# Wider moving operands for the attention values, shorter stationary operands in three HGRN levels

## The chip, the cores and the metric

The kernel runs on one core of a Trainium2 chip. The metric is the device time of one launch in microseconds; times are given as the median of several runs. The engines are named as in the profile: PE (TensorE matmuls), PEld (its weight loads), DVE (VectorE), ACT (ScalarE), POOL (GpSimd) and SP (SyncE, which issues the DMAs here).

## What is computed

The reference is one layer of a decoder trunk on 256 tokens and 1024 channels. A normed input is projected to 3072 columns, which feed three groups of token mixers: a gated linear recurrence (LRU, 256 channels), an HGRN2 group (4 heads of 64) and an attention group (8 heads of 64). The three results are concatenated, projected back, added to the input, and passed through a squared-ReLU MLP.

```python
h = rms_norm(x, norm_mix[l])
z = jnp.einsum('bsd,de->bse', h, w_in[l])
a_x, a_y, b_q, b_f, b_i, b_g, c_q, c_k, c_v = jnp.split(z, split_at, axis=-1)
ya = rglru_group(a_x, a_y, ...)
yb = hgrn2_group(b_q, b_f, b_i, b_g, lower_bounds[l], hg_norm_w[l])
yc = moba_group(c_q, c_k, c_v)
y = jnp.concatenate([rms_norm(ya, ...), yb, rms_norm(yc, ...)], axis=-1)
x = x + jnp.einsum('bse,ed->bsd', y, w_out[l])
h = rms_norm(x, norm_mlp[l])
u = jnp.square(jax.nn.relu(jnp.einsum('bsd,df->bsf', h, w_ff1[l])))
x = x + jnp.einsum('bsf,fd->bsd', u, w_ff2[l])
```

With 256 tokens the attention has a single key block, so it is causal softmax attention with a linear bias. `c_v`, the values, are the last 512 of the 3072 columns.

## The kernel before, in words

**Arithmetic.** Each large product is made of three fp32r matmuls (`mm3`, lines 299 to 303): high half by high half, high by low, low by high. Every weight chunk of 1 MB (128 partitions of 2048 numbers) is loaded by SP into one of three `raw` buffers and split in two halves by `split_w` (line 96, `S_` in the plan): a cast on ACT (line 71), then a subtraction on DVE (line 72). The split's second half also issues the load three chunks ahead.

**Order.** Everything before the MLP is written out by hand. `slots` (line 830) is a list of 84 pieces of matmul work: 48 quarters of the input projection (`in_quarter`, four for each of 12 chunks), 32 parts of the output projection (`wout_part`) and 4 first parts of the MLP. Ahead of a slot stand the steps that `plan` (line 835) gives for it. Each engine runs its own instructions strictly in the order in which slots and steps issue them; semaphores keep data in order across engines. PSUM is eight banks, handed out first freed, first used (`mis`, line 48; `free`, line 61).

**Values of the attention.** Chunks 10 and 11 of the input projection (slots 40 to 47) are the two halves of the value columns, 256 columns each with all eight contraction tiles. The tokens are stationary and the weights move (line 313): for a quarter, four contraction tiles by three matmuls of 256 moving columns. Each chunk takes one bank; `at_v` (line 624) brings it out on ACT with two activations of 256 columns, through `z_tok` (line 243).

**Attention.** For each head, `at_mm` makes scores, `at_max` (DVE) adds the bias and takes the maximum, `at_exp` (ACT, lines 652 and 653) exponentiates, `at_nrm` (DVE, lines 667 and 669) divides, `at_tr` (PE, line 658) transposes the probabilities, `at_pt` (ACT, line 662) brings them out, and `at_av` (PE, lines 673 to 682) multiplies a pair of heads by the values. Then come `at_sq`, `at_sum`, `at_ss`, `at_rms`, `at_bc`, `at_y` and `at_split` for the group's norm. Pairs 0 and 1 of `at_av` stand ahead of slot 46, ahead of the transpose of head 7; pairs 2 and 3 stand ahead of slot 50. `at_ss` stands ahead of slot 53 and `at_bc`, which needs its result by way of DVE and POOL, ahead of slot 56.

**HGRN levels.** `hg_mm(L)` (lines 390 to 405) makes the attention of a block of tokens on the block before it, for L = 1, 2, ..., 64. It has eight products of 64 stationary rows by 128 stationary columns (keys) by 64 moving columns (queries), in f32; the trace shows each as two matmuls, so 16 a level. The two head halves use partitions 0 to 63 and 64 to 127. `hg_pred` reads the result; for L of 16 and more it reads rows `2*L*n` to `2*L*n + L`, so never the last L.

Of the kernel before, what the change touches and what calls it, by code (L numbers as in the profile page):

```python
# [11 lines left out]
AF = mybir.ActivationFunctionType  # L12
# [3 lines left out]
P = 128  # L16
S = 256
D = 1024
KT = D // P
# [13 lines left out]
def trunk_kernel(ctx: ExitStack, tc, x, x_t, w_in, w_out, w_ff1, w_ff2, small, hg_norm, norm_final, out):  # L33
    nc = tc.nc
    V, A, G, T = nc.vector, nc.scalar, nc.gpsimd, nc.tensor
# [12 lines left out]
    def mis(name):  # L48
        b = idle.pop(0)
        held[name] = (b,)  # L50
        return banks[:, b, :]

    def mis2(name):
        age = {b: n for n, b in enumerate(idle)}
        b = min((b for b in (0, 2, 4, 6) if b in age and b + 1 in age), key=lambda b: max(age[b], age[b + 1]))
        idle.remove(b)
        idle.remove(b + 1)
        held[name] = (b, b + 1)
        return banks[:, b:b + 2, :]

    def free(name):
        idle.extend(held.pop(name))

    def wt(name, shape, tag=None, bufs=None, dt=F32):
        return work.tile(shape, dt, name=name, tag=tag or name, bufs=bufs)
# [11 lines left out]
    NI = len(in_order)  # L77
# [9 lines left out]
    raw, hi_w, lo_w = {}, {}, {}  # L87
# [68 lines left out]
    hTh, hTl = hT[:, :, 0, :], hT[:, :, 1, :]  # L156
# [30 lines left out]
    for L in LEVELS:  # L187
        n = 64 // L
        m = const.tile([P, n, L], F32, name=f"lmask{L}")
# [24 lines left out]
    rx = wt("rx", [P, 2])  # L214
# [28 lines left out]
    def z_tok(i, dst, func=AF.Copy):  # L243
        for t in range(2):
            A.activation(dst[:, t, :], z[i][t], func, scale=rx[:, t:t + 1])
        free(f"z{i}")
# [52 lines left out]
    def mm3(o, l, r, first, last):  # L299
        (lh, ll), (rh, rl) = l, r  # L300
        T.matmul(o, lh, rh, start=first, stop=False)  # L301
        T.matmul(o, lh, rl, start=False, stop=False)  # L302
        T.matmul(o, ll, rh, start=False, stop=last)  # L303

    def in_mm(i, half, k):
        o = z[i][half]
        s_ = slice(half * 128, (half + 1) * 128)
        wh = hi_w[i].rearrange("p (k c) -> p k c", c=CW)[:, k, :]
        wl = lo_w[i].rearrange("p (k c) -> p k c", c=CW)[:, k, :]
        if in_order[i][1] == CH:  # L310
            mm3(o, (wh[:, s_], wl[:, s_]), (hTh[:, k, :], hTl[:, k, :]), k == 0, k == KT - 1)
        else:
            mm3(o, (hTh[:, k, s_], hTl[:, k, s_]), (wh, wl), k == 0, k == KT - 1)

    def in_quarter(i, q):
        if q == 0:
            if i < 2:
                z[i] = [mis(f"z{i}{b}")[:, 0:256] for b in range(2)]
            else:
                a = mis(f"z{i}")  # L320
                z[i] = [a[:, 0:256], a[:, 256:512], a]
        if i < 2:
            for k in (2 * q, 2 * q + 1):
                for half in range(2):
                    in_mm(i, half, k)
        else:
            for k in range(4 * (q % 2), 4 * (q % 2) + 4):
                in_mm(i, q // 2, k)
# [7 lines left out]
    kB = wt("kB", [P, 2, 256])  # L336
# [53 lines left out]
    def hg_mm(L):  # L390
        ps = ps_h[L] = mis2(f"lv{L}")
        halves = [slice(0, 64), slice(64, 128)]
        if L == 128:
            for hp in range(2):
                for par, r in enumerate(halves):
                    T.matmul(ps[:, par, hp * 128:(hp + 1) * 128], kB[r, hp, 0:128], qd[r, hp, 128:256],
                             start=True, stop=True)
            return
        for hp in range(2):
            for half in range(2):  # L400
                g = 2 * hp + half
                hs = slice(half * 128, (half + 1) * 128)
                for par, r in enumerate(halves):
                    rhs = qd[r, hp, hs].rearrange("p (n w) -> p n w", w=2 * L)[:, :, L:]
                    T.matmul(ps[:, par, g * 64:(g + 1) * 64], kB[r, hp, hs], rhs, start=True, stop=True)  # L405

    att_g = att_d.rearrange("p (g a) t -> p a g t", a=2)

# [205 lines left out]
    cv = wt("cv", [P, 2, 512])  # L614
# [6 lines left out]
    def at_k(g):  # L621
        zT(6 + 2 * g, ck[g])

    def at_v(g):
        z_tok(10 + g, cv[:, :, g * 256:(g + 1) * 256])

    def at_bias(h):
        sc_t[h] = wt("sc", [P, 384], tag="sc", bufs=3)
# [192 lines left out]
    def x1_ss():  # L821
        for t in range(2):
# [5 lines left out]
    nfb = wt("nfb", [P, D], tag="oc")  # L828
    S_ = split_w
    slots = [(in_quarter, i, 2 * h + q) for h in range(2) for i in range(2) for q in range(2)]  # L830
    slots += [(in_quarter, i, q) for i in range(2, NI) for q in range(4)]
    slots += [(wout_part, k, t, n) for k in range(4) for t, n in tn]
    slots += [(wout_part, k, t, n) for t, n in tn for k in range(4, 8)]
# [18 lines left out]
        16: [(S_, 6, 1)],  # L852
        17: [(hg_dqk,), (lr_x,)],
        18: [(hg_mm, 1), (S_, 5, 1), (lr_conv, 1)],
        19: [(hg_up, 1), (lr_conv, 0), (hg_gate_act,)],
        20: [(lr_y_ev,)],
        21: [(hg_mm, 2)],
        22: [(hg_up, 2)],
        23: [(hg_diag,), (lr_gate_mm, "i"), (hg_pred, 1), (S_, 7, 0), (S_, 7, 1)],
        24: [(lr_y_sq,), (lr_gate_mm, "r"), (S_, 8, 0), (lr_gate_act, "r"), (at_q, 0), (hg_pred, 2)],  # L860
        25: [(lr_gate_act, "i"), (lr_ix,), (hg_gate_dve,)],
        26: [(lr_y_in,), (lr_th,), (hg_mm, 4), (S_, 9, 0)],
        27: [(hg_up, 4), (hg_pred, 4), (lr_y_tanh,)],
        28: [(S_, 8, 1), (lr_y_gelu,)],
# [15 lines left out]
        41: [(at_bias, 7), (hg_av,), (at_tr, 3), (at_nrm, 4), (at_max, 7), (lr_split,)],  # L880
        42: [(at_tr, 4), (at_pt, 2), (at_pt, 3), (S_, 12, 1)],
        43: [(at_exp, 5), (at_exp, 6), (at_nrm, 5), (S_, 11, 1), (hg_sq,), (at_nrm, 6), (hg_rms,)],
        44: [(at_pt, 4), (at_tr, 5), (at_v, 0), (S_, 13, 0), (at_exp, 7), (at_nrm, 7)],
        46: [(at_av, 0), (at_av, 1), (at_tr, 7), (hg_out,), (at_sq, 0), (at_sq, 1), (at_pt, 7)],
        47: [(at_tr, 6), (at_pt, 5), (at_sum, 0, 1)],
        48: [(x_load,), (at_pt, 6), (at_v, 1)],
        50: [
            (hg_tr,), (at_av, 2), (at_av, 3), (S_, 13, 1), (S_, 14, 0), (at_sq, 2), (at_sum, 0, 2), (at_sq, 3),
            (at_sum, 0, 3),
        ],  # L890
        52: [(hg_split,), (S_, 14, 1)],
        53: [(at_ss,), (at_rms,)],
        56: [(at_bc,), (at_rl,), (at_y, 0), (at_y, 1), (at_split, 0), (at_y, 2), (at_y, 3), (at_split, 1)],
        60: [(S_, 15, 0), (S_, 15, 1)],
        64: [(S_, 16, 0)],
# [21 lines left out]
    i = FI + 2  # L917
# [154 lines left out]
```

## Time and profile before

| | |
|---|---|
| median of 3 runs | 315.19 us (314.99 to 316.1) |
| the profiled execution's own time | 316.03 us |
| its span on the core | 314.2 us, so 1.8 us lie around it |
| granted TensorE clock, mean of the span | 0.994 |
| PE, DVE, ACT, POOL busy | 305.0, 210.0, 173.6, 35.5 us |
| bytes moved | 55.68 MB, 177 GB/s on average |

Times in the rows are microseconds from the start of the span. In a timeline row the first number is the start and the second the length of the instruction, or of a run of alike instructions (`x16`); a bracket tells how long the engine sat idle before it, and what ended that. A matmul's length in the record holds the pipeline's latency: back-to-back matmuls overlap, so the step from one start to the next, and not the length, is what one costs.

### The profile page before, as it was taken

The page shows a single profiled execution, that of the slowest core. Times are in us where ns is not written, and L with a number is a line of the kernel's source. Part 1 is how long each engine was busy: PE and PEld are TensorE (multiplying, and loading weights), DVE is VectorE, ACT ScalarE, POOL GpSimd, SP SyncE. Part 2 cuts the span into 40 slices and gives each one's busy share as a digit, 9 for nine tenths or more (in the row PEclk, how much of TensorE's full clock was granted, in tenths as well). Part 3 has the DMA queues.
Part 4 walks back from the last instruction along what each step waited for, and adds up shares of the span by engine and source line. Part 5 has one row for each costly group of instructions (what it writes and reads, how often), then busy time and mean ns, then how long its engine had stood idle before and what let it go on. Part 6 is the DMA issues. An engine that isn't in the chain of part 4 may idle for free.

```text
span 314.2 us, 4805 instructions
## 1 busy us (share of the span) xinstructions
PE 305.0 (97%) x1892; PEld 267.5 (85%) x1892; DVE 210.0 (67%) x339; ACT 173.6 (55%) x292; POOL 35.5 (11%) x83
## 2 busy tenths in 40 slices
PE   8899999999999999999999999999999999999991
PEld 7899989999999788888888888888888888888881
DVE  1748999995766674686866745755764674575573
ACT  3859599783775560666544643552562464355241
POOL 8428700001403000000000000000000000000000
PEclk9999999999999999999999999999999999999997
DMA  7997463342028427047774366246336525621003
GB/s 199 398 367 272 154 262 133 136 153 116 0 73 333 150 117 267 3 145 322 258 278 181 107 247 250 91 197 267 131 138 267 195 94 247 257 92 55 0 12 124
DMA packets 9959, 55.68 MB, mean 177 GB/s; under 512 B 1232, under 2 KB 1488, under 8 KB 4048
## 3 DMA queue, kind: packets, MB, share of 16 engines
q1 hardware_dynamic: 9216, 54.06, 45.9%
q10 hardware_dynamic: 720, 1.31, 1.3%
q8 instruction: 15, 0.25, 0.3%
q14 instruction: 8, 0.07, 0.1%
HBM read 54.32 MB, written 1.05 MB: 176 GB/s over the span
## 4 chain that ended last, share of the span: by engine, by line
PE 82%; DMA 6%; DVE 5%; ACT 3%; issue 2%; SPq 0%; POOLq 0%; POOL 0%; DVEq 0%
PE banks L779 19%; PE banks L301 16%; PE banks L302 15%; PE banks L303 15%; PE banks L780 10%; DMA raw<-in_w_in_dram 6%; DVE wl L72 3%; PE banks L405 2%; ACT wh L71 1%; PE banks L640 1%; PE banks L658 1%; PE banks L681 1%; PE banks L168 1%; PE banks L458 1%; PE banks L521 1%
## 5 line engine op out<-in xcount | busy, mean ns | idle before, releaser
L72 DVE TENSOR_TENSOR wl<-raw,wh 128x1024 fp32r<-128x1024 f32 (+1 forms) x100 | 113.9, 1185 | 23.3 <-ACT wh L71 23.3
L71 ACT CAST wh<-raw 128x1024 fp32r<-128x1024 f32 (+1 forms) x100 | 95.6, 1012 | 5.0 <-DMA raw<-in_w_in_dram 3.8
L779 PE MATMUL banks<-x1c,wh 128*128 128x512 f32 x256 | 91.2, 399 | 0.0
L780 PE MATMUL banks<-x1c,wl 128*128 128x256 f32 x256 | 71.8, 280 | 0.0
L779 PEld LDWEIGHTS banks<-x1c,wh 128*128 128x128 f32 x256 | 48.1, 188 | 12.0 <-DVE x1c L176 0.2
L302 PE MATMUL banks<-wl,uh 128*128 128x512 f32 (+1 forms) x132 | 51.2, 388 | 0.0
L303 PE MATMUL banks<-wh,ul 128*128 128x512 f32 (+1 forms) x132 | 51.1, 387 | 0.0
L301 PE MATMUL banks<-wh,uh 128*128 128x512 f32 (+1 forms) x132 | 51.1, 387 | 0.0
L780 PEld LDWEIGHTS banks<-x1c,wl 128*128 128x128 f32 x256 | 48.3, 189 | 0.6
L791 ACT COPY fb<-banks 128x256 f32<-128x256 f32 x32 | 11.9, 374 | 60.8 <-PE banks L780 60.7
L793 DVE TENSOR_TENSOR fs<-banks,fb 128x256 f32<-128x256 f32 x32 | 13.3, 423 | 41.6 <-ACT fb L791 41.6
L301 PE MATMUL banks<-hT,wh 128*128 128x256 f32 x128 | 37.6, 293 | 0.6 <-ACT hT L161 0.6
L302 PE MATMUL banks<-hT,wh 128*128 128x256 f32 x128 | 36.4, 284 | 0.3 <-DVE hT L162 0.3
L303 PE MATMUL banks<-hT,wl 128*128 128x256 f32 x128 | 36.3, 283 | 0.0
L303 PEld LDWEIGHTS banks<-wh,ul 128*128 128x128 f32 x132 | 24.9, 188 | 5.5 <-DVE ul L797 0.2
L301 PEld LDWEIGHTS banks<-wh,uh 128*128 128x128 f32 x132 | 24.9, 188 | 5.5
L302 PEld LDWEIGHTS banks<-wl,uh 128*128 128x128 f32 x132 | 24.8, 188 | 4.8
L301 PEld LDWEIGHTS banks<-hT,wh 128*128 128x128 f32 x128 | 24.5, 192 | 1.2 <-ACT hT L161 0.8
L302 PEld LDWEIGHTS banks<-hT,wh 128*128 128x128 f32 x128 | 24.5, 191 | 0.7 <-DVE hT L162 0.5
L303 PEld LDWEIGHTS banks<-hT,wl 128*128 128x128 f32 x128 | 24.5, 191 | 0.1
L978 POOL TENSOR_TENSOR r<-v,nhalf 128x1 f32<-128x1 f32 x2 | 1.1, 553 | 199.4 <-DVE v L974 199.4
L796 ACT CAST uh<-fu 128x512 fp32r<-128x512 f32 x16 | 9.9, 620 | 22.8 <-DVE fu L795 22.8
(195 smaller groups left out, 409.6 us busy)
## 6 DMA issues: line engine op xcount, KB each, us to landing
raw<-in_w_ff_dram SPq DMA_DIRECT2D x32, 1024.0 KB, 4.9
raw<-in_w_in_dram SPq DMA_DIRECT2D x10, 1024.0 KB, 5.7
raw<-in_w_out_dram SPq DMA_DIRECT2D x4, 1024.0 KB, 4.9
raw<-in_w_in_dram ACTq DMA_DIRECT2D x4, 256.0 KB, 7.4
xtok<-in_x_dram SPq DMA_DIRECT2D x2, 512.0 KB, 8.3
xa<-in_x_dram SPq DMA_DIRECT2D x2, 512.0 KB, 6.8
xa<-in_x_t_dram SPq DMA_DIRECT2D x3, 256.0 KB, 6.5
raw<-in_w_in_dram SPq DMA_DIRECT2D x2, 256.0 KB, 8.3
```

The costliest lines, as they stand in the source:

```text
L71: A.copy(hi, src)
L72: V.tensor_tensor(lo, src, hi.bitcast(F32), op=OP.subtract)
L168: T.transpose(pair[n % 2][:, i * 256 + t * 128:i * 256 + (t + 1) * 128], src[:, t, (k0 + n) * P:(k0 + n + 1) * P], ident)
L301: T.matmul(o, lh, rh, start=first, stop=False)
L302: T.matmul(o, lh, rl, start=False, stop=False)
L303: T.matmul(o, ll, rh, start=False, stop=last)
L405: T.matmul(ps[:, par, g * 64:(g + 1) * 64], kB[r, hp, hs], rhs, start=True, stop=True)
L779: T.matmul(o, wh[:, k, cs], flat(x1c[:, k]), start=k == 0, stop=False)
L780: T.matmul(o[:, 0:S], wl[:, k, cs], x1h[:, k, :], start=False, stop=k == KT - 1)
L791: A.copy(b[:, c, :], ff1_ps[j, c][:, S:])
L793: V.tensor_tensor(s_[:, c, :], ff1_ps[j, c][:, 0:S], b[:, c, :], op=OP.add)
L796: A.copy(uh[j], u)
```

## The change

The weights of the values are laid out by contraction halves: chunk 10 is contraction tiles 0 to 3 by all 512 value columns, chunk 11 tiles 4 to 7. A quarter is then two contraction tiles by three matmuls of 512 moving columns, for one token half, `t = q // 2`. The banks `v0` and `v1` are taken at slots 40 and 42 and hold both token halves until slots 46 and 48. `at_v` is one activation of 512 columns for a token half; the first moves from the steps of slot 44 to those of slot 46. All four pairs of `at_av` stand ahead of slot 50, behind the transposes of the HGRN result, with their `at_sq` and `at_sum` between them. `at_ss` and `at_rms` move from slot 53 to slot 54. In `hg_mm` the levels 16, 32 and 64 take 112, 96 and 64 stationary columns.

```diff
+    vps = {}
+
+    def v_quarter(i, q):
+        t = q // 2
+        if i == NI - 2 and q % 2 == 0:
+            vps[t] = mis(f"v{t}")
+        s_ = slice(t * 128, (t + 1) * 128)
+        for kk in (2 * (q % 2), 2 * (q % 2) + 1):
+            k = 4 * (i - NI + 2) + kk
+            wh, wl = [w[i].rearrange("p (k c) -> p k c", c=512)[:, kk, :] for w in (hi_w, lo_w)]
+            mm3(vps[t], (hTh[:, k, s_], hTl[:, k, s_]), (wh, wl), k == 0, k == KT - 1)
+
     def in_quarter(i, q):
+        if i >= NI - 2:
+            v_quarter(i, q)
+            return
...
-                    T.matmul(ps[:, par, g * 64:(g + 1) * 64], kB[r, hp, hs], rhs, start=True, stop=True)
+                    m = P - L if L >= 16 else P
+                    T.matmul(ps[0:m, par, g * 64:(g + 1) * 64], kB[r, hp, half * 128:half * 128 + m], rhs,
+                             start=True, stop=True)
...
-    def at_v(g):
-        z_tok(10 + g, cv[:, :, g * 256:(g + 1) * 256])
+    def at_v(t):
+        A.activation(cv[:, t, :], vps[t], AF.Copy, scale=rx[:, t:t + 1])
+        free(f"v{t}")
...
-        44: [(at_pt, 4), (at_tr, 5), (at_v, 0), (S_, 13, 0), (at_exp, 7), (at_nrm, 7)],
-        46: [(at_av, 0), (at_av, 1), (at_tr, 7), (hg_out,), (at_sq, 0), (at_sq, 1), (at_pt, 7)],
-        47: [(at_tr, 6), (at_pt, 5), (at_sum, 0, 1)],
+        44: [(at_pt, 4), (at_tr, 5), (S_, 13, 0), (at_exp, 7), (at_nrm, 7)],
+        46: [(at_tr, 7), (hg_out,), (at_v, 0), (at_pt, 7)],
+        47: [(at_tr, 6), (at_pt, 5)],
         48: [(x_load,), (at_pt, 6), (at_v, 1)],
         50: [
-            (hg_tr,), (at_av, 2), (at_av, 3), (S_, 13, 1), (S_, 14, 0), (at_sq, 2), (at_sum, 0, 2), (at_sq, 3),
-            (at_sum, 0, 3),
+            (hg_tr,), (S_, 13, 1), (S_, 14, 0), (at_av, 0), (at_sq, 0), (at_av, 1), (at_sq, 1), (at_sum, 0, 1),
+            (at_av, 2), (at_sq, 2), (at_sum, 0, 2), (at_av, 3), (at_sq, 3), (at_sum, 0, 3),
         ],
         52: [(hg_split,), (S_, 14, 1)],
-        53: [(at_ss,), (at_rms,)],
+        54: [(at_ss,), (at_rms,)],
```

The host lays out `w_in` to match; the bytes of each load stay the same.

## Rows read from the trace of the kernel before

**Rows 1.** The page's busy times, and its chain that ended last by engine.

```profile
PE 305.0 (97%) x1892; PEld 267.5 (85%) x1892; DVE 210.0 (67%) x339; ACT 173.6 (55%) x292; POOL 35.5 (11%) x83
...
PE 82%; DMA 6%; DVE 5%; ACT 3%; issue 2%; SPq 0%; POOLq 0%; POOL 0%; DVEq 0%
```

**Rows 2.** Waits (who for whom: us in total, times, longest): PE's longest after its start-up.

```profile
PE banks L405 <- DVE kB L432: 0.5, 1, 0.5
```

**Rows 3.** Timeline of PE: 23 starts in slots 44 and 45, nine in the output projection.

```profile
93.47 0.28 PE L302 MATMUL banks<-wl,hT 128*128 128x256 f32 x1
...
96.09 0.28 PE L303 MATMUL banks<-wh,hT 128*128 128x256 f32 x1
...
110.08 0.39 PE L302 MATMUL banks<-wl,yTh 128*128 128x512 f32 x1
...
111.92 0.39 PE L301 MATMUL banks<-wh,yTh 128*128 128x512 f32 x1
```

**Rows 4.** Timeline of PE: both blocks of value products, and what follows each.

```profile
96.30 1.52 PE L681 MATMUL banks<-PT,cv 128*64 128x256 f32 x16
97.75 0.55 PE L658 MATMUL banks<-ident,pr 128*128 128x128 f32 x3
...
103.26 1.52 PE L681 MATMUL banks<-PT,cv 128*64 128x256 f32 x16
104.71 0.50 PE L301 MATMUL banks<-wh,yTh 128*128 128x512 f32 x1
```

**Rows 5.** Weight loads by source line: count, duration in ns (min/median/max), first and last start.

```profile
L405 PEld LDWEIGHTS banks<-qd,kB x112: 182/188/188, 35.8 to 74.7; 64*128 64x128 f32 x112
...
L681 PEld LDWEIGHTS banks<-PT,cv x32: 133/137/137, 96.3 to 104.4; 128*64 128x64 f32 x32
```

**Rows 6.** Timeline of PE: HGRN levels 4 and 64, and what follows each.

```profile
52.10 1.11 PE L405 MATMUL banks<-qd,kB 64*128 64x64 f32 x16
53.14 0.39 PE L301 MATMUL banks<-hT,wh 128*128 128x256 f32 x1
...
73.94 1.11 PE L405 MATMUL banks<-qd,kB 64*128 64x64 f32 x16
74.88 0.33 PE L640 MATMUL banks<-ck,cq 64*128 64x128 f32 x2
```

**Rows 7.** Timeline of ACT: the copy behind the transpose of head 3.

```profile
88.60 0.48 ACT L662 COPY PT<-banks 128x384 f32<-128x384 f32 x1 [1.83 <-PE banks L658]
```

**Rows 8.** Timeline of DVE up to head 7's division; then what the transposes waited for.

```profile
92.76 1.23 DVE L72 TENSOR_TENSOR wl<-raw,wh 128x1024 fp32r<-128x1024 f32 x1 [0.74 <-ACT wh L71]
...
94.53 0.55 DVE L669 TENSOR_SCALAR pr<-pr,ri 128x128 f32<-128x128 f32 x2 [0.47 <-DVE ri L667]
...
95.79 1.23 DVE L72 TENSOR_TENSOR wl<-raw,wh 128x1024 fp32r<-128x1024 f32 x1
...
97.20 0.55 DVE L669 TENSOR_SCALAR pr<-pr,ri 128x128 f32<-128x128 f32 x2
...
  DVE pr L669: 0.2, 1
```

**Rows 9.** Timelines of ACT, PE and POOL: second half's values; the norm's sum, root, broadcast.

```profile
101.53 0.84 ACT L245 ACTIVATE cv<-banks,rx 128x256 f32<-128x256 f32 x2 [0.96 <-PE banks L303]
...
106.88 0.55 PE L697 MATMUL banks<-ones,osq_c 128*128 128x64 f32 x4
...
108.46 0.70 POOL L152 TENSOR_TENSOR crr<-crv,nhalf 128x2 f32<-128x2 f32 x1 [9.91 <-DVE crv L151]
...
109.41 0.61 PE L707 MATMUL banks<-ident,crr 128*128 128x128 f32 x4
```

**Rows 10.** Windows: busy PE, PEld, DVE, ACT, POOL, granted clock, DMA; then the opening matmuls.

```profile
308.00:310.00 2.00, 0.00 (x0) 0.00 (x0) 1.26 (x5) 0.34 (x1) 0.56 (x1) 1.00 0.00 0
310.00:312.00 2.00, 0.00 (x0) 0.00 (x0) 0.54 (x2) 0.38 (x1) 0.00 (x0) 0.61 0.52 184
...
L146 PE MATMUL banks<-ident 128*128 128x128 f32 x24 | 5.4, 425 | 1.4 <-POOL ident masks.py:199 1.4
```

More of the change, by code (lines that the diff above doesn't have):

```diff
@@ L1051 @@
         "x_t": np.concatenate([rows, i["x"].reshape(S, KT, P).transpose(2, 1, 0).reshape(P, KT * S)], axis=1),
-        "w_in": i["w_in"][0].reshape(8, P, 12, 256).transpose(2, 1, 0, 3).reshape(12, P, 2048),
+        "w_in": np.concatenate([
+            i["w_in"][0].reshape(8, P, 12, 256)[:, :, :10].transpose(2, 1, 0, 3).reshape(10, P, 2048),
+            i["w_in"][0][:, 2560:].reshape(2, 4, P, 512).transpose(0, 2, 1, 3).reshape(2, P, 2048)]),
         "w_out": i["w_out"][0].reshape(4, 2, P, 1024).transpose(0, 2, 1, 3).reshape(4, P, 2048),
```

## Prediction

> **What bounds the kernel now.** I read the page's busy times first: PE is busy in 97% of the span, and PE work makes 82% of the chain that ended last [rows 1]. The list of waits is next: once the work has started, PE's longest wait is 0.5 us [rows 2]. So PE sets the time, and what the change takes off PE counts, as long as ACT and DVE keep up. Whether they do is read from the timelines of PE, ACT and DVE side by side in slots 40 to 56, some 84 to 110 us into the span. There one thing stands out. The transpose of head 7 starts on PE at 97.75 [rows 4]; the division that it needs is DVE's last row and ends at 97.20 + 0.55 = 97.75 [rows 8]. The profile even puts 0.2 us of idle time ahead of a transpose down to that line [rows 8]. The two arrive together; PE has nothing to spare there.
>
> **Value matmuls.** A matmul's length in the record says little (0.28 us for 256 moving columns, 0.39 for 512); the step between starts is the price. Of 256 columns, 22 steps take 96.09 - 93.47 = 2.62 us, 0.119 each; of 512, eight steps take 111.92 - 110.08 = 1.84 us, 0.230 each [rows 3]. Before, the values take 2 chunks x 4 quarters x 4 tiles x 3 = 96 matmuls, 11.42 us. Afterwards 48, 11.04 us. That saves 0.38 us, 0.05 a quarter: the columns stay, half the instructions' overhead goes. By the lengths it would seem to be 8 us, which is the trap here. The wider operand needs no new bytes and no new split: the same halves of chunk 11 are wanted at the same slots 44 and 45. The bank that `v1` takes at slot 42 was `z9`'s, which ACT had to read for `hg_av`, and PE has that behind it by slot 41. Cost of both: nothing.
>
> **Value products in one block.** A block of two head pairs holds PE from the last projection matmul at 96.09 to the transpose at 97.75 [rows 3, 4], 1.66 us where 0.12 would do: 1.54 us go from ahead of the transpose of head 7. Behind `hg_tr` two more pairs come in. A block takes 1.45 us from its start to the next work's start [rows 4], with entering and leaving; the record of 1.52 less the pipeline's 0.16 (0.28 - 0.12 above) is 1.36, with entering alone. I take 1.30 for two pairs without either; bounds 1.25 and 1.45. In sum PE saves about 0.25 us, one entry and exit.
>
> **HGRN levels.** A weight load is recorded with 188 ns for 128 columns and 137 for 64 [rows 5], 51 ns for 64 columns or 0.80 ns a column. Sixteen matmuls take 1.04 us with their switch [rows 6], about 0.11 us for a pair of matmuls on the two partition halves. The moving operand has only 64 columns, so the load is what sets that step, and it should fall with the columns: 8 pairs x (16 + 32 + 64) columns x 0.80 = 0.72 us; in proportion to the 0.11 us step it is 8 x 0.11 x 112/128 = 0.77. I take 0.75. No row shows 112 or 96 columns, nor 64 rows by 64 columns, so the bounds are wide: 0 if the step is set by something else, 0.9 with the first, uncovered loads counted twice. This gain reaches PE undiminished: from the wait of 0.5 us [rows 2] up to slot 41 the timelines show PE waiting for nothing, and ACT's rows are released by PE.
>
> One doubt is about form. A level followed by a product of full height holds PE from 52.10 to 53.14, 1.04 us; level 64, followed by scores that also use 64 rows, 73.94 to 74.88, 0.94 [rows 6]. So changing form costs 0.1 us or a little more. The Trainium skill (TensorEngine Tiling (Array Packing), Key Properties) says that a change of tiling mode, not just of tile, drains TensorE. By that rule level 64, now 64 by 64, may no longer share the scores' form, and would give back 0.1 to 0.2 us; the sum would be about 315.75 instead of 315.6. No row shows such a form, so my sum leaves it out.
>
> **What is late next.** Without `at_av` ahead of it, PE reaches the transpose of head 7 sooner, counted from the transpose of head 3: 1.54 us, and 5 x 0.05 = 0.25 for slots 41 to 45, together 1.79. Does the division come sooner? ACT waits 1.83 us for the transpose of head 3, starts its copy at 88.60 [rows 7], and then works without a gap: a cast, two heads' exponentials, the cast of chunk 11's second half. DVE waits 0.74 us for that cast, and from 92.76 to 97.75 it is busy with two splits, heads 6 and 7, and the HGRN sum, with one pause of 0.47 [rows 8]. Taking `at_v` out of ACT's queue in slot 44 helps neither: DVE does not wait for ACT after 92.76. So the division is tied to the transpose of head 3, which moves by 0.75 + 0.05 = 0.80 us, and no more. **PE must then wait about 1.8 us for DVE** (1.4 if the pause of 0.47 does not recur). Behind it, on PE, stand slots 46 and 47, the output projection, and all that follows.
>
> **Other moves.** `at_v(1)` must end before the first `at_av`, not the third. It ends at 101.53 + 0.84 = 102.37, and the block starts at 103.26 [rows 4, 9], 0.9 us of cover that stays, since both follow slot 47; `at_v(0)`, moved from slot 44 to 46, is wanted no sooner. The squares and the sum of pairs 0 and 1 move with their products; ACT and DVE have the four slots of 6 x 0.115 = 0.69 us between the block and `at_ss` for all of them. `at_ss` to `at_bc` was 109.41 - 106.88 = 2.53 us; with two slots between them it is 1.84. The root on POOL ended at 108.46 + 0.70 = 109.16, 2.28 us after `at_ss` began [rows 9]. Of that the four products take 0.55 and POOL 0.70; the other 1.03 us are DVE's step and its queue. If the queue is as long as before, PE waits 2.28 - 1.84 = 0.44 us; if it is empty, nothing. I take nothing, since `at_ss` comes a slot later while the split ahead of DVE's step does not. No DMA issue is moved past another on SP or POOL, and each is released by the same split as before.
>
> **The sum**, from the end of slot 40 on. The transpose of head 7 starts 0.80 us sooner than before (wait included); slots 46 and 47 take 0.10 less; the block is 1.30 longer. -0.80 - 0.10 + 1.30 = **+0.4 us**. After that PE is dense to the end, and the rest moves along. The other way round: 1.4 us of PE work less, 1.8 us of waiting more. On the profiled execution (span 314.2, own time 316.03, which is 0.84 over the median) that gives 316.4; on the median of 315.19 it gives **315.6**. With the pause of 0.47 gone it is 315.15; with the form change and a gain of half from the levels, 316.1.
>
> **Rivals.**
>
> *The wait isn't there.* If DVE's last rows are not what holds the transpose, or they come sooner by some idle time that I take for work, PE keeps all 1.4 us: 313.8. For it: in the profile PE loses at most 0.2 us to that line. Against: DVE's rows are back to back and end at the very start of the transpose [rows 4, 8]. Chance 0.12.
>
> *The levels do nothing.* If the step of 0.11 us is an issue rate and not the load, the 0.75 us stay: 316.3. For it: no row has the new forms. Against: the record of a load is shorter with 64 columns [rows 5]. Chance 0.11.
>
> *Slower: the wait lowers the clock.* Ahead of the transpose of head 7 PE would stand still for about 1.8 us. After the last matmul, with PE idle, the granted clock is 1.00 from 308 to 310 and 0.61 from 310 to 312, on its way from 2.4 to 1.2 GHz [rows 10]. It decides as soon as the clock has fallen to the lower level when the transpose starts. The price: after the standstill at the beginning 24 matmuls of 128 columns held PE for 5.4 us, 0.22 each [rows 10], where three transposes of that size take 0.55 with the latency of 0.16 in it, 0.13 each [rows 4]: 24 x 0.09 = 2.2 us lost. 315.6 + 2.2 = 317.8, over the measurement's doubt. Against: an idle PE kept the full clock from 308 to 310 [rows 10], and after the wait of 0.5 us [rows 2] matmuls ran on at their usual step. Chance 0.07.
>
> **How the numbers follow.** My forecast has 0.70 and lies between 315.1 and 316.2. A measurement of this kernel can tell about 0.5%, 1.6 us, from no change, so the bounds are 313.6 and 316.8. Nothing in the first case or the second passes these, except at the tail of "the wait isn't there", if the levels give their upper bound (0.06), and of "the levels do nothing", if the root's wait of 0.44 us comes on top (0.04). Faster 0.06, slower 0.07 + 0.04 = 0.11, no difference 0.83. The range takes in both rivals that lie within the bounds and leaves out the clock: 313.8 to 316.6.
>
> **What would show it.** Right: an idle stretch of PE of 1.4 to 1.8 us ahead of the transpose at line 658 behind slot 45, released by line 669 on DVE; 48 value matmuls about 0.23 us apart; the blocks of levels 16, 32 and 64 shorter by about 0.1, 0.2 and 0.4 us; one block of 32 value products of some 2.7 us; the block 0.9 us sooner than at 103.26, and the first output part behind it 0.4 us later than at 104.71 [rows 4]. Wrong: no such idle stretch and a span of 312.8; a granted clock under 1 near 97 us; level blocks of unchanged length; a wait ahead of line 707.

## The result, and the profile after

The changed kernel takes 317.29 us (median of 5 runs, 316.91 to 317.61) beside 315.24 us for the kernel before (5 runs, 314.99 to 316.1). The ratio is 1.0056, with a 95% interval of 1.0044 to 1.0068. So the change costs 2.05 us, where the prediction had 0.4 us, and the time lies outside its range, above 316.6. The profiled execution of the changed kernel took 317.29 us, with a span of 315.6.

The changed file is longer, so its lines have moved: the levels are L421 (L405 before), scores L658 (640), the transposes L676 (658), the division L687 (669), the value products L699 (681), the squares L707 (689), `at_ss` L715 (697), `at_bc` L725 (707), the transposes of the HGRN result L504 (487). L707 is thus `at_bc` before and the square after.

First the busy times on the page of the kernel after, beside [rows 1]:

```profile
PE 304.3 (96%) x1844; PEld 263.7 (84%) x1844; DVE 210.0 (67%) x339; ACT 173.6 (55%) x290; POOL 36.1 (11%) x83
```

PE has 48 matmuls fewer and is busy for 0.7 us less, in a span that is 1.4 us longer. So time was not added as work; it was added as waiting. The view of the waits of the kernel after (who for whom: us in total, times, longest) has two lines for PE that the kernel before does not have:

```profile
PE banks L676 <- DVE pr L687: 1.4, 1, 1.4
PE banks L699 <- ACT osq_c L707: 1.0, 2, 0.5
```

The first is the wait for the division of head 7, which was predicted. The second was not: twice, PE waits in the value products for ACT's square of an earlier pair (`at_sq`). Idle time there is counted from the modelled end of the matmul before, so the steps between starts, in the timeline of PE of the kernel after, tell what the waits cost:

```profile
41.21 1.19 PE L421 MATMUL banks<-qd,kB 64*128 64x64 f32 x16
...
61.06 1.00 PE L421 MATMUL banks<-qd,kB 64*112 64x64 f32 x16
62.00 0.39 PE L301 MATMUL banks<-hT,wh 128*128 128x256 f32 x1
...
65.82 0.82 PE L421 MATMUL banks<-qd,kB 64*96 64x64 f32 x16
66.57 0.39 PE L301 MATMUL banks<-hT,wh 128*128 128x256 f32 x1
...
72.95 0.68 PE L421 MATMUL banks<-qd,kB 64*64 64x64 f32 x16
73.56 0.93 PE L658 MATMUL banks<-ck,cq 64*128 64x128 f32 x8
74.42 0.71 PE L611 MATMUL banks<-ident,lrr 128*128 128x128 f32 x4
...
86.75 0.50 PE L676 MATMUL banks<-ident,pr 128*128 128x128 f32 x3
...
92.14 0.39 PE L302 MATMUL banks<-wl,hT 128*128 128x512 f32 x1
...
94.44 0.39 PE L303 MATMUL banks<-wh,hT 128*128 128x512 f32 x1
96.23 0.70 PE L676 MATMUL banks<-ident,pr 128*128 128x128 f32 x3 [1.41 <-DVE pr L687]
96.69 0.47 PE L301 MATMUL banks<-wh,hT 128*128 128x512 f32 x1
...
101.25 0.60 PE L504 MATMUL banks<-ident,ob 128*128 128x128 f32 x4
101.78 0.87 PE L699 MATMUL banks<-PT,cv 128*64 128x256 f32 x8
103.13 1.52 PE L699 MATMUL banks<-PT,cv 128*64 128x256 f32 x16 [0.49 <-ACT osq_c L707]
105.14 0.87 PE L699 MATMUL banks<-PT,cv 128*64 128x256 f32 x8 [0.48 <-ACT osq_c L707]
105.94 0.50 PE L301 MATMUL banks<-wh,yTh 128*128 128x512 f32 x1
...
108.83 0.55 PE L715 MATMUL banks<-ones,osq_c 128*128 128x64 f32 x4
...
110.67 0.61 PE L725 MATMUL banks<-ident,crr 128*128 128x128 f32 x4
```

The starts of the kernel before that rows 1 to 10 did not have are these, from its timeline of PE:

```profile
41.90 1.20 PE L405 MATMUL banks<-qd,kB 64*128 64x64 f32 x16 [0.46 <-DVE kB L432]
...
61.76 1.11 PE L405 MATMUL banks<-qd,kB 64*128 64x64 f32 x16
62.80 0.39 PE L301 MATMUL banks<-hT,wh 128*128 128x256 f32 x1
...
66.62 1.00 PE L405 MATMUL banks<-qd,kB 64*128 64x64 f32 x16
67.56 0.39 PE L301 MATMUL banks<-hT,wh 128*128 128x256 f32 x1
...
75.69 0.71 PE L594 MATMUL banks<-ident,lrr 128*128 128x128 f32 x4
...
88.06 0.50 PE L658 MATMUL banks<-ident,pr 128*128 128x128 f32 x3
...
98.06 0.36 PE L301 MATMUL banks<-wh,hT 128*128 128x256 f32 x1
...
102.73 0.60 PE L487 MATMUL banks<-ident,ob 128*128 128x128 f32 x4
```

The profiled execution of the kernel before was late by 0.69 us when it came to HGRN level 2, where nothing had been changed yet; its wait of 0.5 us [rows 2] belongs to that. So the last column below leaves these 0.69 us out; it is what the change did.

| start on PE | before | after | shift | shift from level 2 on |
|---|---|---|---|---|
| level 2 | 41.90 | 41.21 | -0.69 | 0 |
| behind level 64 and its scores | 75.69 | 74.42 | -1.27 | -0.58 |
| transposes of head 3 | 88.06 | 86.75 | -1.31 | -0.62 |
| transposes of head 7 | 97.75 | 96.23 | -1.52 | -0.83 |
| first matmul of slot 46 | 98.06 | 96.69 | -1.37 | -0.68 |
| transposes of the HGRN result | 102.73 | 101.25 | -1.48 | -0.79 |
| output part behind the value products | 104.71 | 105.94 | +1.23 | +1.92 |
| `at_bc` | 109.41 | 110.67 | +1.26 | +1.95 |

Up to the HGRN result's transposes the changed kernel is 0.79 us ahead. Then the stretch from there to the output part behind the value products takes 2.71 us more than before, where the prediction had 1.30, and that stands to the end. The block of 32 products holds PE from 101.78 to 105.94, 4.16 us, in three pieces of 8, 16 and 8. Beside it the squares in the timeline of ACT of the kernel after:

```profile
102.69 0.39 ACT L707 ACTIVATE osq_c<-banks 128x256 f32<-128x256 f32 x1
104.05 0.38 ACT L707 ACTIVATE osq_c<-banks 128x256 f32<-128x256 f32 x1 [0.97 <-PE banks L699]
104.70 0.38 ACT L707 ACTIVATE osq_c<-banks 128x256 f32<-128x256 f32 x1 [0.27 <-PE banks L699]
```

The first square ends at 102.69 + 0.39 = 103.08 and the products of pair 1 start at 103.13; the third ends at 105.08 and the products of pair 3 start at 105.14. Between them, the products of pair 2 start without a wait. In `at_av` pairs 0 and 1 write the two halves of one bank, pairs 2 and 3 those of the next:

```python
def at_av(c):
    if c % 2 == 0:
        av = mis(f"av{c // 2}")
        ps_o[c], ps_o[c + 1] = av[:, 0:256], av[:, 256:512]
    ...
```

### The profile page after: what moved, and what is told of

Its sections match the earlier page's. It is cut to its first block, busy times and chain, and to the rows that moved or that the text cites. A ratio compares the mean times of both kernels' runs of the same rounds, so it can differ in the third digit from the quotient of the medians.

```text
span 315.6 us, 4707 instructions
## 1 busy us (share of the span) xinstructions
PE 304.3 (96%) x1844; PEld 263.7 (84%) x1844; DVE 210.0 (67%) x339; ACT 173.6 (55%) x290; POOL 36.1 (11%) x83
## 3 DMA queue, kind: packets, MB, share of 16 engines
q10 hardware_dynamic: 720, 1.31, 1.3%
## 4 chain that ended last, share of the span: by engine, by line
PE 90%; DVE 2%; DMA 2%; issue 2%; ACT 2%; POOLq 0%; POOL 0%; DVEq 0%; ACTq 0%
PE banks L797 19%; PE banks L301 18%; PE banks L302 18%; PE banks L303 18%; PE banks L798 10%; DMA raw<-in_w_in_dram 2%; PE banks L421 2%; PE banks L658 1%; PE banks L699 1%; PE banks L676 1%; DVE wl L72 1%; PE banks L168 1%; PE banks L475 1%; PE banks L538 1%; ACT wh L71 0%
```

## The experiments

The theory after this reading: the change lost time in two waits that its new order makes. One is PE's wait for the division of head 7 (no value products ahead of it any more); the other is that the squares stand between the products, so that PE may not write the second half of a bank until ACT has read the first. The rivals: the value products are dearer by themselves in a block of four, whatever stands between them; and the head 7 wait only moves a loss that would appear later anyway. The first four kernels ran beside the kernel before at a median of 315.6 us, the other four beside 315.33. They are compared by their ratios to it, since the time before differed a little from one to the other.

**The squares behind the products.** Step 50 of the changed kernel, with the four products back to back:

```diff
-            (hg_tr,), (S_, 13, 1), (S_, 14, 0), (at_av, 0), (at_sq, 0), (at_av, 1), (at_sq, 1), (at_sum, 0, 1),
-            (at_av, 2), (at_sq, 2), (at_sum, 0, 2), (at_av, 3), (at_sq, 3), (at_sum, 0, 3),
+            (hg_tr,), (S_, 13, 1), (S_, 14, 0), (at_av, 0), (at_av, 1), (at_av, 2), (at_av, 3), (at_sq, 0), (at_sq, 1),
+            (at_sum, 0, 1), (at_sq, 2), (at_sum, 0, 2), (at_sq, 3), (at_sum, 0, 3),
```

> The changed kernel with the four pairs of value products issued back to back and all squares and sums behind them. Theory (a square on ACT reads the half of a PSUM bank whose other half the next pair writes, and PE waits for it, twice 0.65 us): both waits go, one block of 32 matmuls of about 2.75 us, 1.3 us less than the changed kernel: 316.0. Rival (the block is slow for another reason, such as four pairs' weights or ACT's two casts ahead): the block stays near 4.1 us, or PE waits as long ahead of line 715, and the time stays at 317.3.

It took 316.06 us, ratio 1.0016 (1.0007 to 1.0025), 0.40% or about 1.3 us better than the change's 1.0056. Its timeline of PE:

```profile
96.10 0.70 PE L676 MATMUL banks<-ident,pr 128*128 128x128 f32 x3 [1.42 <-DVE pr L687]
...
101.65 2.82 PE L699 MATMUL banks<-PT,cv 128*64 128x256 f32 x32
104.41 0.50 PE L301 MATMUL banks<-wh,yTh 128*128 128x512 f32 x1
```

The block is one piece again and takes 104.41 - 101.65 = 2.76 us, 1.40 less than in the changed kernel. The prediction's two terms for it were 1.45 and 1.30, 2.75 together. So the block of four pairs has the price that was given to it, and the rival falls; 1.40 us were the squares between. The wait for head 7 is still there.

**The same order, but other banks.** The squares stay between the products, and pairs 0 and 2 share one bank, 1 and 3 the other, so that neighbours in the order never share one:

```diff
-        if c % 2 == 0:
-            av = mis(f"av{c // 2}")
-            ps_o[c], ps_o[c + 1] = av[:, 0:256], av[:, 256:512]
+        if c < 2:
+            av = mis(f"av{c}")
+            ps_o[c], ps_o[c + 2] = av[:, 0:256], av[:, 256:512]
...
-        if c % 2:
-            free(f"av{c // 2}")
+        if c >= 2:
+            free(f"av{c - 2}")
```

> The changed kernel with squares and products interleaved as they are, but neighbouring pairs in different banks: pairs 0 and 2 share one, 1 and 3 the other. Theory (the shared bank makes the wait): pair 1 no longer waits for the square of pair 0; pair 2 waits for it at most 0.1 to 0.2 us, since that square has the time of pair 1 (0.65 us) to run; about 1.1 us less than the changed kernel, 316.2. Rival (issuing ACT's squares between PE's products costs it, whatever the bank): 317.3.

It took 315.98 us, ratio 1.0014 (1.0005 to 1.0024). From its timeline of PE:

```profile
101.83 2.88 PE L699 MATMUL banks<-PT,cv 128*64 128x256 f32 x32
104.64 0.50 PE L301 MATMUL banks<-wh,yTh 128*128 128x512 f32 x1
```

And from its timeline of ACT:

```profile
102.75 0.38 ACT L707 ACTIVATE osq_c<-banks 128x256 f32<-128x256 f32 x1
103.40 0.39 ACT L707 ACTIVATE osq_c<-banks 128x256 f32<-128x256 f32 x1 [0.27 <-PE banks L699]
```

The squares run at the same places in the order, 0.65 us apart, while PE goes on: 2.81 us for the block. The order alone does not cost the time; the shared bank does. The Trainium skill (PSUM — Partial Sum Buffer, PSUM bank collisions raise a hardware error) says that semaphores are to guard PSUM by bank and quadrant of partitions and not by address. These two runs agree: with the two halves of one bank PE waited 0.70 us a time for ACT, with different banks it did not. The program's tile (`banks`) is all eight banks, so the wait is not one for the whole tile. It ends when ACT's square does; whether the memory itself would have held PE up, without the program's semaphores, no run here shows.

**Head 7 later.** The transposes of head 7 and the copy behind them go from step 46 to the end of step 48, behind those of head 6:

```diff
-        46: [(at_tr, 7), (hg_out,), (at_v, 0), (at_pt, 7)],
+        46: [(hg_out,), (at_v, 0)],
...
-        48: [(x_load,), (at_pt, 6), (at_v, 1)],
+        48: [(x_load,), (at_pt, 6), (at_v, 1), (at_tr, 7), (at_pt, 7)],
```

> The changed kernel with the transpose of head 7 and its copy moved from the steps of slot 46 to the end of those of slot 48, behind slot 47. Theory (PE waits there 1.6 to 1.8 us for DVE's division and has other work to do meanwhile): the wait goes, 1.6 us less than the changed kernel, 315.7; the two waits inside the block stay. Rival (the wait is only handed on, to the transposes of the HGRN result, to the values or to the products): the idle time shows up behind slot 47 and the time stays near 317.3.

It took 315.73 us, ratio 0.9999 (0.999 to 1.0009), 0.57% or 1.8 us better than the change. Its timeline of PE:

```profile
97.99 0.49 PE L676 MATMUL banks<-ident,pr 128*128 128x128 f32 x3
...
100.25 0.87 PE L699 MATMUL banks<-PT,cv 128*64 128x256 f32 x8
101.60 1.52 PE L699 MATMUL banks<-PT,cv 128*64 128x256 f32 x16 [0.48 <-ACT osq_c L707]
103.60 0.87 PE L699 MATMUL banks<-PT,cv 128*64 128x256 f32 x8 [0.48 <-ACT osq_c L707]
```

The transposes no longer wait, and the two waits in the block are as they were. So the head 7 wait was a loss of its own, which nothing later took back, and it was not unavoidable: with two more slots of projection work ahead of the transposes, DVE is in time.

**Both.**

> Both edits: squares behind all products, head 7 behind slot 47. Theory (the three waits are all that the change costs, and they are independent): 1.3 + 1.6 = 2.9 us less than the changed kernel, 314.4, which is 0.8 us under the kernel before; PE has no wait over 0.2 us behind slot 40. Rival (with these gone the next one binds: the sum's root on POOL ahead of the broadcast, or the HGRN transposes): 315 or more.

The edits of the first and the third together took 314.53 us, ratio 0.9961 (0.9949 to 0.9974). The gains add up: 0.40% and 0.57% alone, 0.95% together. From its timeline of PE:

```profile
100.48 2.82 PE L699 MATMUL banks<-PT,cv 128*64 128x256 f32 x32
...
107.96 0.61 PE L725 MATMUL banks<-ident,crr 128*128 128x128 f32 x4
```

Behind slot 40 no wait of PE is left that the view of waits lists. Against the kernel before the gain is 0.39%, 1.2 us. The parts give the same: 0.58 us from the levels as measured, and by the prediction's terms 0.38 from the wide value matmuls and 0.25 from one block instead of two, 1.21 together. So the arithmetic of the change is worth that, and the order in which it came lost it and 2 us more.

**The levels alone.** The kernel before with the hunk of `hg_mm` and nothing else.

> The kernel before with the shorter stationary operands of levels 16, 32 and 64 alone. Theory (the step of a level is set by the weight load, and the gain reaches the end): 0.6 us less by what the three blocks lost in the changed kernel's trace, 314.6. Rival (the gain is lost to a wait that PE meets sooner, at the transpose of head 7 or elsewhere): 315.2.

It took 314.9 us, ratio 0.9985 (0.9976 to 0.9994), 0.5 us faster. The view of its lines, shapes apart (busy us, mean ns of one, idle before), shows the new forms, level 64's among them:

```profile
L406 PE MATMUL banks<-qd,kB 64*64 64x64 f32 x16 | 0.7, 224 | 0.0
```

In its trace level 4 starts at 51.57 us, the work behind level 64's scores at 74.57 and `at_bc` at 108.30. Against 52.10 [rows 6], 75.69 and 109.41 [rows 9] that is a gain of 0.59 us from level 4 to the scores, and of 0.58 to `at_bc`. So what the levels save reaches the end, and the rival that they do nothing falls.

**Head 7 first, in the kernel before.** The same loss made by itself: the two product steps go behind the transposes of head 7.

```diff
-        46: [(at_av, 0), (at_av, 1), (at_tr, 7), (hg_out,), (at_sq, 0), (at_sq, 1), (at_pt, 7)],
+        46: [(at_tr, 7), (at_av, 0), (at_av, 1), (hg_out,), (at_sq, 0), (at_sq, 1), (at_pt, 7)],
```

> The kernel before with one swap in the steps of slot 46: the transpose of head 7 ahead of the products of pairs 0 and 1. Nothing else changes. Theory (DVE's division is ready only when the block of products is over, so the block is what covers it): PE waits about 1.5 us ahead of the transpose and the time goes up by 1.5 us, to 316.7. Rival (the division is ready earlier and only looks late): 315.2.

It took 317.57 us, ratio 1.0067 (1.0055 to 1.008). Its timeline of PE:

```profile
97.50 0.70 PE L658 MATMUL banks<-ident,pr 128*128 128x128 f32 x3 [1.19 <-DVE pr L669]
```

Without the 1.45 us of products ahead of it, PE stands idle for the same division. In the trace `at_bc` is 110.97 - 109.41 = 1.56 us later, about what was expected; the medians differ by 2.2 us. The two profiled executions, 317.55 and 316.03 us, differ by 1.52, as the traces do; that of the kernel before lies 0.7 us above its median of 315.33, that of this kernel at its median. Both traces come to level 2 late (41.85 and 41.90 us). If the usual execution of this kernel starts late and that of the kernel before does not, that would be the difference; how often either does was not tried.

**A square between two products, in the kernel before.** Only pairs 2 and 3, so that there is one such wait:

```diff
-            (hg_tr,), (at_av, 2), (at_av, 3), (S_, 13, 1), (S_, 14, 0), (at_sq, 2), (at_sum, 0, 2), (at_sq, 3),
-            (at_sum, 0, 3),
+            (hg_tr,), (S_, 13, 1), (S_, 14, 0), (at_av, 2), (at_sq, 2), (at_sum, 0, 2), (at_av, 3), (at_sq, 3),
+            (at_sum, 0, 3),
```

> The kernel before with the square of pair 2 and its sum issued between the products of pairs 2 and 3, behind the two casts, as the changed kernel does. Theory (pair 3 waits for the square that reads its bank): one wait of about 0.65 us inside the second block, 0.65 us more, 315.9. Rival (no wait without four pairs in one go): 315.2.

It took 316.42 us, ratio 1.0033 (1.002 to 1.0046). Its timeline of PE:

```profile
103.16 0.87 PE L681 MATMUL banks<-PT,cv 128*64 128x256 f32 x8
104.52 0.87 PE L681 MATMUL banks<-PT,cv 128*64 128x256 f32 x8 [0.48 <-ACT osq_c L689]
```

One wait, of the same length as those of the changed kernel. In the trace `at_bc` starts 110.03 - 109.41 = 0.62 us later, and level 4 at 52.01 instead of 52.10, so it makes 0.71 us; the profiled executions, 316.73 and 316.03 us, differ by 0.70 too. The medians differ by 1.1, again some 0.4 more than the traces show, and again left open.

**72 columns in level 64.** Beside the waits, the levels had given 0.58 us and not 0.75. If a 64 by 64 form is another form than the scores' 64 by 128, then eight columns more keep the form and save the switch. The edit stands on the kernel with both orders mended:

```diff
-                    m = P - L if L >= 16 else P
+                    m = max(P - L, 72) if L >= 16 else P
```

> The kernel of e4 with 72 instead of 64 stationary columns in level 64. Theory (with 64 rows by 64 columns the level has another form than the scores behind it, and the switch costs about 0.15 us; with over 64 columns it keeps their form): the switch goes, the eight pairs of loads take 8 x 8 columns x 0.84 ns = 0.05 us more, so 0.1 us less than e4 in the trace, from the level's first matmul to the last of the scores; too little for the times to tell. Rival (no such switch): 0.05 us more.

It took 314.25 us, ratio 0.9965 (0.9953 to 0.9977); by the ratios it can't be told from the kernel with 64 columns. The timeline of PE tells more:

```profile
73.14 0.73 PE L421 MATMUL banks<-qd,kB 64*72 64x64 f32 x16
73.71 0.88 PE L658 MATMUL banks<-ck,cq 64*128 64x128 f32 x8
74.51 0.71 PE L611 MATMUL banks<-ident,lrr 128*128 128x128 f32 x4
```

From the level's first matmul to the work behind the scores it is 74.51 - 73.14 = 1.37 us. With 64 columns it is 74.42 - 72.95 = 1.47, though each matmul loads less; before it was 75.69 - 73.94 = 1.75. Eight columns more should have cost 8 pairs x 8 x 0.80 ns [rows 5], 0.05 us; they saved 0.10. So the 64 by 64 form itself costs about 0.15 us ahead of these scores; between 64 and 72 columns no other width was tried.

## Why the prediction was wrong

**The step that failed** is the sentence on the squares: "The squares and the sum of pairs 0 and 1 move with their products", with a cost of nothing. It asked whether ACT and DVE would have the squares and sums done in time for `at_ss`, and they had: `at_ss` to `at_bc` takes 110.67 - 108.83 = 1.84 us without a wait, as predicted. It did not ask what the next product on PE must wait for. So the block's term, 1.30 us with bounds of 1.25 and 1.45, came out as 2.71. Before, both pairs of a bank were written before either was squared; the diff puts a square between them, and that wait has no row in the trace of before, since the order never made it. Two such waits cost 1.40 us (the block with the squares between less the block without). A price could be had ahead of time. The bank is in `at_av`, and in the trace of before two squares of 256 columns take 0.66 us and begin 0.05 us behind the recorded end of the products, 103.26 + 1.52 = 104.78 [rows 4]:

```profile
104.83 0.66 ACT L689 ACTIVATE osq_c<-banks 128x256 f32<-128x256 f32 x2 [0.57 <-PE banks L681]
```

With the latency of 0.16 us that the prediction took off a block's record, this gives an estimate of 0.16 + 0.05 + 0.33 = 0.54 us a wait; 0.70 was measured.

**The block** itself was right: 2.76 us measured without the squares, 2.75 by the prediction's terms.

**The value matmuls** were right. Ten steps with 512 moving columns take 94.44 - 92.14 = 2.30 us, 0.230 each, the step taken from [rows 3]. The banks and splits moved with them show no wait.

**The wait for head 7** was right, and is the other half of the result. DVE's rows of the kernel after stand in the same order as in [rows 8], pause included:

```profile
93.23 0.55 DVE L687 TENSOR_SCALAR pr<-pr,ri 128x128 f32<-128x128 f32 x2 [0.49 <-DVE ri L685]
...
95.89 0.55 DVE L687 TENSOR_SCALAR pr<-pr,ri 128x128 f32<-128x128 f32 x2
```

The division ends at 96.44 instead of 97.75, 1.31 us sooner, exactly as much as the transposes of head 3, to which it was said to be tied. PE could have gone on one step behind 94.44, at 94.67, and goes on at 96.23, 1.56 us later. The rest of the wait lies inside the transposes: the first needs only the first of the division's two instructions and starts before 96.44, the other two need the second, so the three take 96.69 - 96.23 = 0.46 us, where those of head 3 take 0.25 (86.75 to 87.00). Together PE loses 1.77 us, where 1.79 was worked out, and the run with head 7 moved gained 1.8. The levels' shortfall is not in this wait, as it moves PE and the division alike; it is in the time at which the division ends: counted from level 2 on, 0.62 us sooner where 0.80 was forecast. Slot 46 follows the division's end by 0.25 us instead of 0.31 and so starts 0.68 us sooner, and slots 46 and 47 save 0.11 where 0.10 was forecast.

**The levels** were mis-sized, 0.58 for 0.75. Level 16 holds PE for 62.00 - 61.06 = 0.94 us instead of 62.80 - 61.76 = 1.04, level 32 for 66.57 - 65.82 = 0.75 instead of 67.56 - 66.62 = 0.94, level 64 for 73.56 - 72.95 = 0.61 instead of 74.88 - 73.94 = 0.94 [rows 6]: 0.10, 0.19 and 0.33, where about 0.1, 0.2 and 0.4 were expected. The scores behind level 64 then take 0.05 more. The price of a column was right: from 128 to 72 columns level 64 and its scores lose 1.75 - 1.37 = 0.38 us, and 8 pairs by 56 columns by 0.80 ns are 0.36. What is missing, 0.17, lies mostly in the form of level 64, about 0.15 by the last run: the doubt that the prediction named and left out of its sum. The Trainium skill (TensorEngine Tiling (Array Packing), Key Properties) says that a change of mode drains TensorE. That 72 columns are cheaper here than 64, by 0.1 us, agrees with it, though no run shows the drain itself. The price of about 0.15 us is within the 0.1 to 0.2 that the prediction named.

**The clock** did not fall. The windows of the kernel after (busy PE, PEld, DVE, ACT, POOL, granted clock, DMA) have it at 1.00, the level of 2.4 GHz, both in the 2 us that hold the wait and in the next, in which the transposes and the first matmuls of slot 46 run:

```profile
94.00:96.00 2.00, 0.82 (x4) 0.36 (x2) 1.86 (x5) 0.79 (x3) 1.34 (x1) 1.00 1.03 385
96.00:98.00 2.00, 1.77 (x9) 1.43 (x10) 1.14 (x4) 0.86 (x2) 1.24 (x1) 1.00 0.97 401
```

So the 317.8 of that rival is near the measured time, which has another cause. The rival without the wait fell with the row of 1.41 us, and the one without a gain from the levels with their shorter blocks.

**The sum** again, with what was measured: -0.68 up to slot 46, -0.11 in slots 46 and 47, and the block 2.71 longer than the block of two pairs, +1.92 us. The forecast was -0.80 - 0.10 + 1.30. Of the 1.52 us between them 1.40 are the squares' two waits, and the other 0.12 are the levels' 0.17 less some 0.05 that slot 46 came sooner behind the division. On the median this gives 317.1 where 317.29 was measured. The range was too narrow for a reason that the sum can't show: the levels, the block and the root's wait had bounds, but the squares, taken at nothing, had none.

## What to carry to other kernels

When an edit puts a reader of a PSUM bank between two writers of it, price a wait for the reader in front of the second writer, even if they touch different halves: write both first, or give neighbours in the order different banks. Work that is moved away from ahead of a dependent instruction may have been its cover, so ask for each moved piece what it stood in front of, and move the dependent instruction too. A smaller operand that changes the array's form can cost more than a slightly larger one that keeps it: here 64 stationary columns cost 0.1 us more than 72, in one place of one kernel.

## What the runs showed that was not expected

- The 64 by 64 form ahead of 64 by 128 products: 72 stationary columns, more to load, came out 0.1 us cheaper than 64 (1.37 us against 1.47, level and scores together; 1.46 or 1.47 in all six traces with 64 columns). That is the fastest kernel of this study by its median, 314.25 us, though not apart from the one with 64 columns by the intervals.
- The wait of a writer for the reader of the other half of a bank: the square is 0.38 to 0.39 us long, but each one costs PE 0.70 us (1.40 for two), since it begins only when the last product is out, and PE restarts 0.05 us behind its end.
- DVE's pause of 0.47 us between a reciprocal and its division [rows 8] came again as 0.49 us at the same place of the plan, and not at the next head's. What makes it was not tried.
- Start-up varies: level 2 began at 41.90 us in the trace of the kernel before and between 41.15 and 41.85 in the nine others, one of each kernel, with nothing changed ahead of it. The medians of the two orders tried on the kernel before moved by 0.4 to 0.7 us more than their traces, though the profiled executions moved as the traces did; whether that is start-up too stays open.
